# Three gating rows spread by transfers through memory in a two-layer decoder block on one Trainium2 core

## Chip, core and metric

The kernel runs on one core of one Trainium2 chip. The metric is the device time of one execution in microseconds; the time before is the median of three runs. In the text, PE is TensorE (PEld its weight load), DVE is VectorE, ACT is ScalarE, POOL is GpSimd, and SP is the sync engine, which here only issues transfers. Each engine works through its own instructions in order; a transfer issued by an engine stands in that engine's queue too, and an issue that waits for a semaphore holds up everything behind it there.

## The reference, cut to what matters

Two layers run over 512 tokens of width 1024. A vector `c` gives, for each layer, six modulation rows of 1024 numbers; two of them, `g1` and `g2`, gate what a mixer and an MLP add to the residual.

```python
c_act = jax.nn.silu(c)
for i in range(DEPTH):                                   # 2 layers
    mod = c_act @ ada_w[i] + ada_b[i]
    sh1, sc1, g1, sh2, sc2, g2 = jnp.split(mod, 6, axis=-1)
    h = modulate(rmsnorm(x, norm_mix_g[i]), sh1, sc1)
    y = pool_mixer(h, ...) if i == 0 else sgu_mixer(h, ...)
    x = x + g1[:, None, :] * y
    h = modulate(rmsnorm(x, norm_mlp_g[i]), sh2, sc2)
    x = x + g2[:, None, :] * (jnp.square(jax.nn.relu(h @ w1[i])) @ w2[i])
return rmsnorm(x, final_g)
```

Three of the four gating rows matter here: `g2` of layer 0 (in the code's column count, `c_g(1, 0)` of `mods[0]`), `g1` of layer 1 (`c_g(0, 0)` of `mods[1]`) and `g2` of layer 1 (`c_g(1, 0)` of `mods[1]`). The remaining one, `g1` of layer 0, is folded into the pooling weights and is not touched.

## The kernel before

Weights arrive as fp32, and every product is made of three fp32r products: `split` (lines 164 to 169) turns a weight tile into a high half `wh` (ACT, line 167) and a low half `wl` (DVE, line 168), and `mm3` (lines 174 to 178) issues wl times high, wh times low and wh times high. A raw weight tile of 512 KB lands in pool `w4`, which has three buffers; the halves `wh` and `wl` have five buffers each, so weights are made some products ahead of PE.

The modulation rows are computed on DVE, not on PE: `ada_tile` (line 190) loads a 128 x 1024 tile of `ada_w` into a buffer of `w4` (line 194) and reduces it against `cb`, the activated `c` on all partitions (line 198), into one column; after each second tile `finish_mods` (line 183) adds the bias and writes two columns of `mods[i]`. A gating row so stands in `mods` as 128 partitions x 8 columns: column k holds elements 128 k to 128 k + 127, one in each partition. But the gate is applied to tokens on the partitions (`gated`, line 964: `tmp = y * gb`), which needs the 1024 numbers along the free dimension, on all partitions: the tile `gb`, 128 x 1024, of which there is one for all three rows.

That is what `spread_cols` is for. `diagonals` (line 207, POOL) makes eight 128 x 128 tiles, each the identity scaled by one column; a product with a matrix of ones (line 216, PE, fp32, two of 128 x 512) sums over the partitions, so that every partition of the result holds all of the row; ACT evicts the two halves into `gb` (line 217). The 128 x 8 x 128 tile of scaled identities takes a buffer of `w4` in two cases, and one called `dgu` of pool `su` in the third.

The order of the stages and where the three spreads stand:

- Pooling mixer of layer 0, then the first MLP blocks (0 to some 90 us).
- MLP of layer 0. `mlp` (from line 595) walks a list `units`: "f" (first product and squared ReLU), "p" and, in layer 1, "s" (products arranged after Strassen's scheme), "q" (the last part). Beside the units it calls a list `extra` one by one at an even pace: eight `ada_tile` calls that finish `g2` of layer 0, the first spread, and 24 `ada_tile` calls for layer 1.
- SGU mixer of layer 1: two passes for `v`, its layer norm on DVE, then `do_u` and `do_mix` in a fixed order ("u0 u1 u2 u3 m0 u4 ..."); `do_u` pops up to three entries of `ex`, the first of which is the second spread. The product with `w_o` follows, with `gated` and eight more `ada_tile` calls.
- MLP of layer 1, which begins with four "f" blocks (`first1`; the transposes of `normed`, line 992, stand in the middle of them). The third spread's identities are made at the start, its products after the block `u == (0, 7)`. The weights of the "p" units come from loads and accumulating loads (`b_of`, line 761; `b_add`, line 765, on POOL).

PE's instructions stand in the order in which the program writes them (`manual_schedule(engines={PE})`). DVE, ACT, POOL and SP are in the program's order only in the opening part; later a list scheduler of the framework orders each of these queues, by its own estimate of durations, so a change in one place can move instructions elsewhere on them.

The input tiles' sources are named after the tensors: `in_ada` for `ada_w`, `in_w1f` for the first blocks of `w1` in layer 1, `in_w_v`, `in_w_u` (tile `ur`) and `in_w_o` for the SGU, `bt` and `b` for `w2`. Lines 1043 to 1045 load the layer norm's rows and the mixing weights of the SGU, one of them (`lnt`) as a broadcast of a row in memory to all partitions, which is the form of transfer that the change uses as well.

Of the kernel before, what the change touches and what calls it, by code (L numbers as in the profile page):

```python
# [7 lines left out]
F32 = mybir.dt.float32  # L8
F32R = mybir.dt.float32r
AF = mybir.ActivationFunctionType  # L10
ALU = mybir.AluOpType
# [3 lines left out]
P = 128  # L15
D = 1024
S = 512
KD = D // P
# [23 lines left out]
def c_sh(n, k):  # L42
    return 24 * n + 2 * k + 1


def c_g(n, k):
    return 24 * n + 16 + k
# [31 lines left out]
def decoder_kernel(ctx: ExitStack, tc: tile.TileContext, xtok, vecs, rows, fgrow, ada0, adag, ada1, pool_w, w1s, w1, w1f, w1b, w2, w2e, w_v, w_u, w_o, wsT, lnp, bs, out):  # L79
    nc = tc.nc  # L80
    V, A, G, T = nc.vector, nc.scalar, nc.gpsimd, nc.tensor
# [3 lines left out]
    w4 = ctx.enter_context(tc.tile_pool(name="w4", bufs=3))  # L85
# [20 lines left out]
    def bank(name, pool=None):  # L106
        pool = pool or ps
        return pool.tile([P, S], F32, name=name, tag="mm" if pool is ps else "xz")
# [4 lines left out]
    ones = cp.tile([P, P], F32, name="ones")  # L113
# [3 lines left out]
    ident = cp.tile([P, P], F32, name="ident")  # L117
    G.memset(ident, 0.0)
    G.affine_select(out=ident, in_=ident, compare_op=ALU.not_equal, fill=1.0, base=0, pattern=[[-1, P]], channel_multiplier=1)
    mods = [cp.tile([P, 48], F32, name=f"mods{i}") for i in range(2)]  # L120
# [16 lines left out]
    gb = big.tile([P, D], F32, name="gb")  # L137

    def X(t):
        return x_[t // 2][:, t % 2]  # L140

    def H(k, c):

        return h_[0][:, 0, k, c], h_[0][:, 1, k, c]
# [4 lines left out]
    def mod(i, c):  # L149
        return mods[i][:, c : c + 1]  # L150
# [30 lines left out]
    def finish_mods(i, b, pm):  # L181

        V.tensor_tensor(mods[i][:, 2 * b : 2 * b + 2], pm, vec[:, V_ADAB + 48 * i + 2 * b : V_ADAB + 48 * i + 2 * b + 2], ALU.add)
        n, q = divmod(b, 12)
        if q < 8:
            g0 = (V_MIX, V_MLP)[n] + 8 * i + q
            V.scalar_tensor_tensor(scl[i][n][:, q : q + 1], mod(i, 2 * b), 1.0, vec[:, g0 : g0 + 1], ALU.add, ALU.mult)
# [3 lines left out]
    def ada_tile(i, t, src, get):  # L191

        r = get()
        nc.sync.dma_start(r, src)
        b, j = divmod(t, 2)
        if j == 0:
            pmv[i, b] = sm.tile([P, 2], F32, name="pmv", tag="pmv")
        V.scalar_tensor_tensor(r, r, 1.0, cb, ALU.mult, ALU.mult, accum_out=pmv[i, b][:, j : j + 1])  # L198
        if j == 1:
            finish_mods(i, b, pmv.pop((i, b)))  # L200
# [1 line left out]
    def get4():  # L202
        return w4.tile([P, D], F32, name="ada", tag="w4")

    def diagonals(dg, cols):
        for k in range(KD):
            G.tensor_scalar(dg[:, k], ident, cols[:, k : k + 1], None, ALU.mult)

    def spread_cols(cols, dg=None):

        if dg is None:
            dg = w4.tile([P, KD, P], F32, name="dg", tag="w4")
            diagonals(dg, cols)
        for n in range(2):
            po = bank("pb")
            T.matmul(po, ones, dg[:, 4 * n : 4 * n + 4], start=True, stop=True)
            A.activation(gb[:, S * n : S * n + S], po, AF.Copy)


    def power(v, n):  # L220
# [12 lines left out]
    with (  # L233
# [67 lines left out]
        def rms():  # L301
            v0 = sm.tile([P, NT], F32, name="rv4", tag="rv4")
            V.tensor_scalar(v0, ss, RMS_EPS, None, ALU.add)
            rt.append(power(v0, NT))
# [285 lines left out]
    def parts(o, a):  # L590

        A.activation(o[0], a, AF.Copy)
        V.tensor_tensor(o[1], a, f32(o[0]), ALU.subtract)  # L593

    def mlp(i, first, extra, last, ending):
# [3 lines left out]
        with (  # L599
# [56 lines left out]
            def a_sums(step):  # L656


                def a(r, j):
                    return h32[0][:, 4 * j : 4 * j + 4, 256 * r : 256 * r + 256]  # L660

                def operand(pool, tag):
                    t = pool.tile([P, 2, 4, 256], F32R, name="as", tag=tag)
                    return t[:, 0], t[:, 1]

                def minus(o, p, q):
                    V.tensor_tensor(o, p, q, ALU.subtract)

                first, half = slice(0, 256), slice(256, 512)
                if step == 0:  # L670
                    sums_a.update({1: H(slice(0, 4), first), 2: H(slice(4, 8), first), 4: H(slice(4, 8), half)})
                    shift(hx, LINE - GAP)
                    minus(a(1, 1), a(1, 0), a(1, 1))
                    m, o = 5, operand(hx, "hx")
                elif step == 1:
                    minus(a(1, 1), a(1, 1), a(0, 0))
                    m, o = 6, operand(big, "x0")
                elif step == 2:
                    minus(a(0, 0), a(0, 0), a(1, 0))
                    V.tensor_tensor(a(1, 1), a(1, 1), a(0, 1), ALU.add)  # L680
                    m, o = 3, operand(big, "x1")
                else:
                    m, o = 7, H(slice(0, 4), half)
                parts(o, a(0, 0) if m == 7 else a(1, 1))
                sums_a[m] = o
# [214 lines left out]

            gain = mods[i][:, c_g(1, 0) : c_g(1, 0) + KD]
            done = first(put)
            if i:
                dg = su.tile([P, KD, P], F32, name="dgu", tag="u")
                diagonals(dg, gain)
            units = [("f", (0, f)) for f in range(done, 8)]
            for c in range(3):
                if i == 0:
# [17 lines left out]
            def ahead(n):  # L926

                if i == 0:
                    return min(n + 3, len(units))
                m, s = n + 1, items(*units[n])  # L930
                while m < len(units) and m < n + 5:
                    s += items(*units[m])
                    if s > 5 and m > n + 1:
                        break
                    m += 1
                return m
# [4 lines left out]
            for n, (kind, u) in enumerate(units):  # L941
                for m in range(n, ahead(n)):
                    if m not in ready:
                        ready[m] = prep[units[m][0]](units[m][1])
                while at < len(extra) and at < due * (n + 1):
                    extra[at]()
                    at += 1
                run[kind](u, ready[n])
                if i and kind == "f":
                    a_sums(u[1] - 4)  # L950
                    if u == (0, 7):
                        spread_cols(gain, dg)
                if i and u == (3, 1, 4):
                    reload()

# [24 lines left out]
    def normed(hf, i, n):  # L980

        xs = []
        for r in range(2):
            t = w4.tile([P, D], F32, name="xs", tag="w4")
            A.activation(t, X(2 * hf + r), AF.Copy, scale=rms(2 * hf + r))
            xs.append(t)
        c = slice(256 * hf, 256 * hf + 256)
        for k in range(0, KD, 2):
            px = bank("px")
            for q in range(2):  # L990
                for r in range(2):
                    T.transpose(px[:, 256 * q + P * r : 256 * q + P * r + P], xs[r][:, P * (k + q) : P * (k + q) + P], ident)
            tt = h32[0][:, k : k + 2, c] if h32 else sm.tile([P, 2, 256], F32, name="tt", tag="tmp")
            for q in range(2):
                a, b = scl[i][n][:, k + q : k + q + 1], mod(i, c_sh(n, k + q))
                if q:
                    A.activation(tt[:, q], px[:, 256:512], AF.Identity, bias=b, scale=a)
                else:
                    V.tensor_scalar(tt[:, q], px[:, 0:256], a, b, ALU.mult, ALU.add)
            parts(H(slice(k, k + 2), c), tt)  # L1000


    h32, xd = [], []
    dram = ctx.enter_context(tc.tile_pool(name="dram", bufs=1, space=bass.MemoryType.DRAM))

    def spill(h):
        xd.append(dram.tile([P, 2, D], F32, name=f"xd{h}"))
# [2 lines left out]
    def reload():  # L1010
        for h in range(2):
            x_[h] = big.tile([P, 2, D], F32, name=f"x{h}", tag=f"x{h}")
            G.dma_start(x_[h], xd[h])
        load_fg()
# [4 lines left out]
        return SWEEP  # L1019

    ex = [lambda q=q: ada_tile(0, 40 + q, ada1[q], get4) for q in range(8)]
    ex += [lambda: spread_cols(mods[0][:, c_g(1, 0) : c_g(1, 0) + KD])]
    ex += [lambda q=q: ada_tile(1, q, ada1[8 + q], get4) for q in range(24)]
    mlp(0, first0, ex, gated, lambda: normed(0, 1, 0))


# [6 lines left out]
    with (  # L1033
# [37 lines left out]
                V.tensor_tensor(v, v, lnt[:, n].rearrange("p (a b) -> p a b", a=2), op)  # L1071

        u, gt, wu = {}, {}, {}
        ex = [lambda: spread_cols(mods[1][:, c_g(0, 0) : c_g(0, 0) + KD])]
        ex += [lambda q=q: ada_tile(1, q, ada1[8 + q], get4) for q in range(24, 40)]

        def do_u(n):
# [75 lines left out]
    def last1(t, c0, n, src, y):  # L1153
# [13 lines left out]
        else:  # L1167
# [5 lines left out]
            nc.sync.dma_start(out[t, :, 1], X(t)[:, S:D])  # L1173

    mlp(1, first1, [], last1, lambda: None)


# [77 lines left out]
```

## Time and profile before

| | before |
|---|---|
| median of 3 runs | 876.26 us (875.87 to 877.03) |
| the profiled execution's own time | 876.84 us |
| its span | 875.1 us |
| PE busy | 858.3 us |
| DVE busy | 682.7 us |
| ACT busy | 449.6 us |
| POOL busy | 55.5 us |
| HBM read | 150.55 MB |

The page shows one execution on the chip. "Busy" is the time in which an engine had an instruction at work; matmuls overlap, so PE busy is not PE at its peak. The page also lists the groups of instructions by line, which the products of the spreads do not reach (they are among the smaller groups). The lines on which the argument rests stand in the prediction, in the part that uses them.

### The profile page before, as it was taken

How to read it: one execution, taken by the hardware profiler on the slowest of the kernel's cores; microseconds unless marked ns; L12 is line 12 of the kernel's file. 1: busy time of each engine (PE TensorE's matmuls, PEld its weight loads, DVE VectorE, ACT ScalarE, POOL GpSimd, SP SyncE). 2: the span in 40 equal slices, each digit the busy share in tenths (PEclk: the TensorE clock that was granted, in tenths of full speed). 3: DMA queues.
4: the chain of work that ended last, by engine and by line, in shares of the span. 5: the costliest groups of instructions: out<-in, count | busy, mean ns of one | idle time of the engine just before them, and what ended most of it. 6: DMA issues, size and time to landing. Idle time of an engine off the chain costs nothing. (4 is left out here: it accounts for less than half of the span.)

```text
span 875.1 us, 11762 instructions
## 1 busy us (share of the span) xinstructions
PE 858.3 (98%) x4580; PEld 739.1 (84%) x4580; DVE 682.7 (78%) x893; ACT 449.6 (51%) x653; POOL 55.5 (6%) x75
## 2 busy tenths in 40 slices
PE   8999999999999999999999999999999999999996
PEld 7778888788888888888878888999999988889885
DVE  6889696788869876657798866776877798778965
ACT  5285755554444445337233336665765575556621
POOL 3000002000000000000410012000000000000001
PEclk9999999999999999999999999999999999999999
DMA  9969843553554442514658526817464547456312
GB/s 348 417 233 310 299 175 122 192 192 129 184 201 160 145 145 72 193 65 177 214 170 266 169 97 224 305 31 188 121 201 126 139 130 247 102 140 216 122 47 97
DMA packets 37789, 155.51 MB, mean 178 GB/s; under 512 B 4195, under 2 KB 4323, under 8 KB 32486
## 3 DMA queue, kind: packets, MB, share of 16 engines
q1 hardware_dynamic: 35282, 137.72, 43.9%
q0 software_dynamic: 2304, 16.78, 8.9%
q8 instruction: 36, 0.59, 0.3%
q10 hardware_dynamic: 148, 0.27, 0.1%
q14 instruction: 19, 0.16, 0.1%
HBM read 150.55 MB, written 4.19 MB: 177 GB/s over the span
## 5 line engine op out<-in xcount | busy, mean ns | idle before, releaser
L176 PE MATMUL po<-hb,wl 128*128 128x256 f32 (+1 forms) x624 | 209.3, 335 | 1.3 <-DVE wl L168 1.3
L178 PE MATMUL po<-hb,wh 128*128 128x256 f32 (+1 forms) x624 | 207.6, 333 | 0.0
L177 PE MATMUL po<-hb,wh 128*128 128x256 f32 (+1 forms) x624 | 207.6, 333 | 0.0
L168 DVE TENSOR_TENSOR wl<-raw,wh 128x1024 fp32r<-128x1024 f32 x107 | 130.9, 1224 | 39.4 <-ACT wh L167 39.0
L167 ACT ACTIVATE wh<-raw 128x1024 fp32r<-128x1024 f32 x107 | 112.7, 1057 | 64.8 <-PE pm L178 28.6
L178 PE MATMUL pm<-wh,oh 128*128 128x512 f32 x336 | 130.7, 389 | 0.0
L177 PE MATMUL pm<-wl,oh 128*128 128x512 f32 x336 | 130.7, 389 | 0.0
L176 PE MATMUL pm<-wh,ol 128*128 128x512 f32 x336 | 130.7, 389 | 0.0
L176 PEld LDWEIGHTS po<-hb,wl 128*128 128x128 f32 x624 | 117.1, 188 | 14.6 <-DVE wl L168 1.7
L177 PEld LDWEIGHTS po<-hb,wh 128*128 128x128 f32 x624 | 117.2, 188 | 13.0 <-issue 0.7
L178 PEld LDWEIGHTS po<-hb,wh 128*128 128x128 f32 x624 | 118.0, 189 | 11.9
L168 DVE TENSOR_TENSOR wl<-b,wh 128x1024 fp32r<-128x1024 f32 x60 | 73.0, 1221 | 24.7 <-ACT wh L167 24.7
L198 DVE SCALAR_TENSOR_TENSOR ada<-ada,cb 128x1024 f32<-128x1024 f32 x56 | 68.3, 1223 | 15.7 <-DMA ada<-in_ada 15.5
L178 PEld LDWEIGHTS pm<-wh,oh 128*128 128x128 f32 x336 | 63.0, 188 | 13.2
L176 PEld LDWEIGHTS pm<-wh,ol 128*128 128x128 f32 x336 | 63.1, 188 | 12.3
L177 PEld LDWEIGHTS pm<-wl,oh 128*128 128x128 f32 x336 | 63.0, 188 | 12.3
L167 ACT ACTIVATE wh<-b 128x1024 fp32r<-128x1024 f32 x60 | 63.0, 1055 | 13.0 <-PE pm L178 6.7
L630 ACT ACTIVATE g<-po 128x512 f32<-128x512 f32 x40 | 23.6, 599 | 75.7 <-PE po L178 73.8
L969 ACT ACTIVATE tmp<-x 128x512 f32<-128x512 f32 (+1 forms) x25 | 15.3, 612 | 63.0 <-DVE x L965 63.0
L857 DVE TENSOR_TENSOR y<-y,pm 128x512 f32<-128x512 f32 x68 | 43.6, 682 | 0.0
L176 PE MATMUL po<-as,wl 128*128 128x256 f32 x144 | 40.7, 283 | 2.9 <-DVE wl L168 1.9
L168 DVE TENSOR_TENSOR wl<-bt,wh 128x1024 fp32r<-128x1024 f32 x24 | 28.9, 1222 | 17.5 <-ACT wh L167 17.5
(211 smaller groups left out, 1491.0 us busy)
## 6 DMA issues: line engine op xcount, KB each, us to landing
ada<-in_ada SPq DMA_DIRECT2D x72, 512.0 KB, 3.3
b<-in_w SPq DMA_DIRECT2D x21, 1024.0 KB, 4.9
raw<-in_w SPq DMA_DIRECT2D x25, 512.0 KB, 3.9
raw<-in_w1b SPq DMA_DIRECT2D x24, 512.0 KB, 5.0
bt<-in_w POOLq DMA_DIRECT2D x9, 1024.0 KB, 8.3
raw<-in_w2e SPq DMA_DIRECT2D x16, 512.0 KB, 3.3
wh<-in_ada SPq DMA_DIRECT2D x9, 512.0 KB, 9.6
wl<-in_ada SPq DMA_DIRECT2D x9, 512.0 KB, 9.9
```

What stands on the lines that cost most here:

```text
L167: A.activation(h, r, AF.Copy)
L168: V.tensor_tensor(l, r, f32(h), ALU.subtract)
L176: T.matmul(o, wl, mh, start=first, stop=False, **kw)
L177: T.matmul(o, wh, ml, start=False, stop=False, **kw)
L178: T.matmul(o, wh, mh, start=False, stop=last, **kw)
L198: V.scalar_tensor_tensor(r, r, 1.0, cb, ALU.mult, ALU.mult, accum_out=pmv[i, b][:, j : j + 1])
L630: A.activation(t, po, AF.Relu)
L857: V.tensor_tensor(yt, yt, banks[hf], ALU.subtract if minus else ALU.add)
L969: A.activation(tmp, xt, AF.Square, scale=D**-0.5, accum_out=s[:, len(cs) : len(cs) + 1])
```

## The change

`spread_cols` now stores the eight columns into a row in device memory (`dram.tile([KD, P])`, one for each of the three spreads) with the two dimensions exchanged, and then loads that row into all partitions of `gb` with a broadcast. Both transfers are issued on SP's queue. The products, the scaled identities with their buffers, and the evictions are gone. The first spread's call moves within `extra` from behind the eighth `ada_tile` to behind the twelfth; the other two stand at the same calls as before. The pool `dram`, which the kernel already used for `spill`, is opened earlier.

```diff
-    def diagonals(dg, cols):
-        for k in range(KD):
-            G.tensor_scalar(dg[:, k], ident, cols[:, k : k + 1], None, ALU.mult)
-
-    def spread_cols(cols, dg=None):
-
-        if dg is None:
-            dg = w4.tile([P, KD, P], F32, name="dg", tag="w4")
-            diagonals(dg, cols)
-        for n in range(2):
-            po = bank("pb")
-            T.matmul(po, ones, dg[:, 4 * n : 4 * n + 4], start=True, stop=True)
-            A.activation(gb[:, S * n : S * n + S], po, AF.Copy)
+    dram = ctx.enter_context(tc.tile_pool(name="dram", bufs=1, space=bass.MemoryType.DRAM))
+
+    def spread_cols(cols, name):
+
+        line = dram.tile([KD, P], F32, name=name)
+        nc.sync.dma_start(line.rearrange("k p -> p k"), cols)
+        nc.sync.dma_start(gb, line.rearrange("(o k) p -> o (k p)", o=1).to_broadcast([P, D]))
...
-            if i:
-                dg = su.tile([P, KD, P], F32, name="dgu", tag="u")
-                diagonals(dg, gain)
...
                     if u == (0, 7):
-                        spread_cols(gain, dg)
+                        spread_cols(gain, "gain1")
...
     ex = [lambda q=q: ada_tile(0, 40 + q, ada1[q], get4) for q in range(8)]
-    ex += [lambda: spread_cols(mods[0][:, c_g(1, 0) : c_g(1, 0) + KD])]
     ex += [lambda q=q: ada_tile(1, q, ada1[8 + q], get4) for q in range(24)]
+    ex.insert(12, lambda: spread_cols(mods[0][:, c_g(1, 0) : c_g(1, 0) + KD], "gain0"))
     mlp(0, first0, ex, gated, lambda: normed(0, 1, 0))
...
-        ex = [lambda: spread_cols(mods[1][:, c_g(0, 0) : c_g(0, 0) + KD])]
+        ex = [lambda: spread_cols(mods[1][:, c_g(0, 0) : c_g(0, 0) + KD], "gainm")]
         ex += [lambda q=q: ada_tile(1, q, ada1[8 + q], get4) for q in range(24, 40)]
```

More of the change, by code (lines that the diff above doesn't have):

```diff
@@ L1003, in decoder_kernel @@
     h32, xd = [], []
-    dram = ctx.enter_context(tc.tile_pool(name="dram", bufs=1, space=bass.MemoryType.DRAM))
     def spill(h):
```

## The prediction

> **What bounds the kernel now.** I read the page first, then the waits of PE, then the busy time by stage, then single rows in order of time. In the rows of a timeline the columns are start, duration, engine, line, operation and tiles, count, and in brackets the idle time before with what ended it; "SPq" is an issue by SP's queue.
>
> ```profile
> span 875.1 us, 11762 instructions
> PE 858.3 (98%) x4580; PEld 739.1 (84%) x4580; DVE 682.7 (78%) x893; ACT 449.6 (51%) x653; POOL 55.5 (6%) x75
> ```
> ```profile
> PE po L176 <- DVE wl L168: 3.1, 3, 1.3
> ```
> ```profile
> 431.00:501.00 70.00, 70.00 (x339) 58.44 (x338) 63.50 (x107) 23.85 (x32) 4.38 (x4) 1.00 0.63 208
> 540.00:560.00 20.00, 19.87 (x175) 19.87 (x176) 13.30 (x19) 12.44 (x19) 3.19 (x5) 1.00 0.95 338
> ```
>
> TensorE is the bound: 98% busy, its longest kind of wait after the opening is 3.1 us in three pieces, and the granted clock is 1.00 in both stretches shown (columns there: stretch, length, then busy PE, PEld, DVE, ACT, POOL, clock, DMA share, GB/s). So time taken off PE's queue comes off the end, unless what feeds PE cannot come earlier. Two stages have such feeders close behind: from 431 to 501 us VectorE is busy 63.5 of 70 us, and from 540 to 560 us the DMA engines are 95% busy.
>
> **What the change removes.** Each of the three spreads is two fp32 products, which PE runs as four passes between two weight products.
>
> ```profile
> 157.26 0.39 PE L178 MATMUL pm<-wh,oh 128*128 128x512 f32 x1
> ...
> 157.94 0.40 PE L178 MATMUL pm<-wh,oh 128*128 128x512 f32 x1
> 158.18 1.88 PE L216 MATMUL pb<-dg,ones 128*128 128x512 f32 x4
> 159.50 0.79 PE L176 MATMUL po<-hb,wl 128*128 128x512 f32 x1
> 160.12 0.40 PE L177 MATMUL po<-hb,wh 128*128 128x512 f32 x1
> ```
> ```profile
> 446.13 0.40 PE L178 MATMUL po<-hb,wh 128*128 128x512 f32 x1
> ...
> 448.31 0.40 PE L177 MATMUL po<-hb,wh 128*128 128x512 f32 x1
> ```
> ```profile
> 585.09 0.28 PE L178 MATMUL po<-hb,wh 128*128 128x256 f32 x1
> ...
> 585.43 0.28 PE L178 MATMUL po<-hb,wh 128*128 128x256 f32 x1
> ...
> 587.38 0.28 PE L177 MATMUL po<-hb,wh 128*128 128x256 f32 x1
> ```
>
> Undisturbed, three 512-wide products start in 157.94 - 157.26 = 0.68 us, so 0.227 each; 256-wide ones in (585.43 - 585.09) / 3 = 0.113. From the last product before a spread to the second one after it there are two such steps. First spread: 160.12 - 157.94 - 0.45 = 1.73 us. Second: 448.31 - 446.13 - 0.45 = 1.73. Third: 587.38 - 585.43 - 0.23 = 1.72. Sum on PE: **5.18 us**. Two slots of PSUM per spread and 24 products on POOL go too, and ScalarE loses six evictions, all beside PE; I give them nothing of their own.
>
> **What it adds: six transfers on SP's queue.** Each spread becomes a store of the 128 x 8 gate columns into a row in memory, whose last step is one 4-byte word (1024 packets, 64 for each of 16 engines), and a load of that row to all partitions (128 x 4 KB), which waits for the store to land and for the last reader of gb. SP is in order, so everything behind them waits too. No row shows a 4-byte packet. The nearest:
>
> ```profile
> q1 hardware_dynamic: 35282, 137.72, 43.9%
> ...
> q10 hardware_dynamic: 148, 0.27, 0.1%
> ```
>
> The columns are packets, MB and share of 16 engines' span. A packet of q1 (3.9 KB) holds an engine for 0.439 x 16 x 875.1 / 35282 = 174 ns, one of q10 (1.8 KB) for about 95 ns. A line through both leaves 26 ns for a packet without bytes; with q10's rounded share at 0.15% it leaves 114. Bounds: nothing, and 174 ns, which is 64 x 0.174 = 11.1 us for a store. I take 40 ns, near the line's end and a little above for that rounding: **2.6 us** in which the rings pass nothing that was issued behind it.
>
> The Trainium skill, "DMA: Bandwidth & Descriptors", says in "Rules for kernel authors" that a last dimension that isn't contiguous becomes one descriptor per element, and in "Specifications" that the engines read, modify and write below 512 B. Its table of measured loads under "Bandwidth" has about 10.5 ns for each packet over all engines at the smallest size; by that, as an estimate, 1024 packets take 10.8 us, which is the upper bound again and speaks against the change.
>
> **First spread (gain0).** In the built order its store stands behind the ninth gather of the stage and ahead of the tenth.
>
> ```profile
> 137.39 0.16 DVE L183 TENSOR_TENSOR mods<-pmv,vec 128x2 f32<-128x2 f32 x1
> ...
> 149.07 1.23 DVE L593 TENSOR_TENSOR ol<-u,oh 128x1024 fp32r<-128x1024 f32 x1 [1.98 <-ACT oh L592]
> ```
> ```profile
> 147.12 0.33 SPq L194 DMA_DIRECT2D ada<-in_ada  x1
> ...
> 155.65 1.07 ACT L167 ACTIVATE wh<-raw 128x1024 fp32r<-128x1024 f32 x1 [0.65 <-PE pm L178]
> ```
>
> The columns are ready at 137.5, while the ninth gather's load was issued at 147.1, because the scaled identities held one of three w4 buffers. That buffer is now free, so the two new transfers use time in which SP only waited. What is late next is the tenth gather, on VectorE ahead of the ol of 149.07. ScalarE's split at 155.65 waited for PE to hand back a buffer, so weights are made ahead of their use; a few us of delay are covered. Price 0; at the upper bound the gather would hold VectorE some 8 us and I would expect a stall of 1 to 2.
>
> **Second spread (gainm).** The store follows the wsbs loads, the load follows two ur loads.
>
> ```profile
> 356.56 0.58 SPq L1045 DMA_DIRECT2D wsbs<-in_bs  x1
> 373.34 19.69 SPq L155 DMA_DIRECT2D raw<-in_w_v  x4
> ...
> 401.35 6.02 SPq L155 DMA_DIRECT2D raw<-in_w_v  x4
> ```
> ```profile
> 397.76 0.69 DVE L964 TENSOR_TENSOR tmp<-y,gb 128x512 f32<-128x512 f32 x1
> ```
>
> SP issues nothing from 357.1 to 373.3, 16 us, above the store's upper bound; gb's last read ends at 398.5, before SP's next issue at 401.4. Price 0. But this stage has VectorE as close feeder:
>
> ```profile
> 500.28 0.69 DVE L1104 TENSOR_TENSOR gtl<-u,gth 128x512 fp32r<-128x512 f32 x1 [0.70 <-ACT gth L1103]
> ```
> ```profile
> 502.26 0.39 PE L176 MATMUL po<-wh,gtl 128*128 128x512 f32 x1
> ```
>
> The last gtl ends at 500.97 and PE takes it at 502.26: 1.29 us of slack, while PE comes 1.73 earlier. VectorE's order is changed here: two of the gathers (1.15 us each) now run before the second split of ur, not after it, which leaves less for the end of the chain. I take 0; bounds 0 and about 2 us, all of this spread's gain and a little more.
>
> **Third spread (gain1).** Its store stands behind three loads of w1f and ahead of bt and the fourth load of w1f; this is the tight place.
>
> ```profile
> 538.56 0.16 DVE L183 TENSOR_TENSOR mods<-pmv,vec 128x2 f32<-128x2 f32 x1
> ...
> 547.30 1.23 DVE L168 TENSOR_TENSOR wl<-raw,wh 128x1024 fp32r<-128x1024 f32 x1 [3.54 <-ACT wh L167]
> 549.06 1.90 DVE L999 TENSOR_SCALAR h<-px,scl,mods 128x256 f32<-128x256 f32 x4 [0.53 <-PE px L992]
> ...
> 553.16 1.29 DVE L593 TENSOR_TENSOR hb<-h,hb 128x512 fp32r<-128x512 f32 x2 [0.66 <-ACT hb L592]
> ```
> ```profile
> 538.90 0.33 SPq L761 DMA_DIRECT2D bt<-in_w  x1
> 540.10 0.33 SPq L155 DMA_DIRECT2D raw<-in_w1f  x1
> ```
> ```profile
> 546.20 1.06 ACT L167 ACTIVATE wh<-raw 128x1024 fp32r<-128x1024 f32 x1 [0.60 <-DMA raw<-in_w1f]
> ```
> ```profile
> 550.08 0.37 PE L176 MATMUL po<-hb,wl 128*128 128x256 f32 x1
> ...
> 555.05 0.28 PE L177 MATMUL po<-hb,wh 128*128 128x256 f32 x1
> ```
>
> The store can go at 538.7, just ahead of bt. The fourth load is what ScalarE waits for at 546.2; VectorE's split of it ends at 548.53, PE wants it at 550.08: slack 1.55. Behind that split VectorE has the scaling at 549.06 (idle 0.53 before it) and the last low half, which ends at 554.45 and is used at 555.05, slack 0.60. So a delay X of that load costs PE about X - 1.1. With X = 2.6: **1.5 us**; with the bounds 0 and 10.0. The broadcast load and two loads of b behind it are wanted later, and what feeds 563 onward was split 5 us ahead; nothing for those.
>
> **Sum.** The profiled execution took 876.84 us (875.1 span and 1.7 around it); the median of the runs is 876.26. 876.84 - 5.18 + 1.5 = 873.2 in that execution's terms, and 876.26 - 3.7 = **872.6** for the median.
>
> **The rivals.**
> 1. The store is cheap, X below 1.1: all 5.18 us stay, 871.1. For it: 4 KB in all, and the line's 26 ns (1.7 us) is not far above. Against: 64 packets per engine.
> 2. VectorE becomes the bound from 431 to 501: the second saving is lost, with up to 0.3 more for gathers that wait in its queue, on top of my sum: 872.6 + 2.0 = 874.6. For it: 63.5 of 70 busy, 1.29 us slack. Against: the moved gathers.
> 3. Slower: the 4-byte packets cost what whole packets cost. At 174 ns the fourth load of w1f is 11.1 us late, PE stands 10.0 us at 550, and the sum is 876.26 - 5.18 + 10.0 = 881.1. It decides from X - 1.1 = 5.18 + 1.75, X = 8.0 us or 125 ns a packet, above the 114 of the line with q10 rounded up. Against it: two kinds of packet suggest that time falls with size. The skill's 10.5 ns (above) would end here, at 880.8 as an estimate.
>
> **How the numbers follow.** My forecast has 0.38 (its own range 871.3 to 874.2, X from 1.3 to 4.2), rival 1 0.15, rival 2 0.17, rival 3 0.22, and 0.08 lies between forecast and rival 3 with no change to tell. What can be told from no change is 0.2%, 1.75 us: faster means below 874.5, slower above 878.0. Rival 2 lies on the line, half and half. Faster 0.38 + 0.15 + 0.09 = 0.62, same 0.08 + 0.08 = 0.16, slower 0.22. The range from 870.6 to 879.5 leaves out a good half of rival 3.
>
> **What would show it.** Right: no L216 on PE, the step from L178 to L177 back at 0.45 us at those three places; PE's start at gt's product about 3.5 us earlier; a stall of 1 to 2 us at the fourth w1f block, with ScalarE waiting longer for that load. Step by step wrong: the store landing in under 3 us or over 8; a stall at the first mixing or the last gtl; SP's w_v loads later than 373 less 1.7; PE idle near 150 to 170. The prediction fails altogether if PE's idle time grows by over 5 us anywhere.

## The result, and the profile after

| | before | after |
|---|---|---|
| median of the runs | 876.64 us (875.87 to 878.36, 4 runs) | 885.26 us (883.25 to 886.68, 4 runs) |
| profiled execution: time, span | 876.84, 875.1 us | 886.36, 884.7 us |
| PE busy | 858.3 us | 856.7 us |
| DMA packets under 512 bytes | 4195 | 7363 |

The kernel became slower: ratio 1.009, 95% interval 1.007 to 1.0109. Line numbers shift a little: the store is line 210, the broadcast load 211, b's loads 755. First the page of the changed kernel, then its table of PE's waits (total in us, times, longest).

```profile
span 884.7 us, 11709 instructions
...
PE 856.7 (97%) x4568; PEld 740.1 (84%) x4568; DVE 680.8 (77%) x893; ACT 446.0 (50%) x647; POOL 34.4 (4%) x51
```
```profile
PE po L176 <- DVE wl L168: 14.5, 4, 10.8
```

PE works less than before, and the span is 9.6 us longer: most of the time went into one wait, 10.8 us long, for a low half of a weight. The next rows, in order of time on SP's queue, ScalarE, VectorE and PE of the changed kernel, follow it back.

```profile
535.17 0.38 SPq L210 DMA_DIRECT2D gain<-mods  x1
535.66 0.52 SPq L755 DMA_DIRECT2D bt<-in_w  x1
536.60 0.33 SPq L155 DMA_DIRECT2D raw<-in_w1f  x1
547.23 0.33 SPq L211 DMA_DIRECT2D gb<-gain  x1
```
```profile
555.17 1.06 ACT L167 ACTIVATE wh<-raw 128x1024 fp32r<-128x1024 f32 x1 [13.27 <-DMA raw<-in_w1f]
```
```profile
556.26 1.23 DVE L168 TENSOR_TENSOR wl<-raw,wh 128x1024 fp32r<-128x1024 f32 x1 [16.19 <-ACT wh L167]
```
```profile
557.54 0.58 PE L176 MATMUL po<-hb,wl 128*128 128x256 f32 x1 [10.82 <-DVE wl L168]
557.92 0.41 PE L177 MATMUL po<-hb,wh 128*128 128x256 f32 x1
...
561.95 0.29 PE L178 MATMUL po<-hb,wh 128*128 128x256 f32 x1
562.07 0.28 PE L176 MATMUL po<-hb,wl 128*128 128x256 f32 x1
...
562.66 0.28 PE L178 MATMUL po<-hb,wh 128*128 128x256 f32 x1
```

The fourth load of w1f is issued at 536.60, right behind gain1's store and bt. ScalarE can split it at 555.17, 18.57 us later; before, issue and split were 6.10 us apart (540.10 and 546.20). So the load came 12.5 us late, and everything behind it on ScalarE, VectorE and PE with it. Behind the stall the products start every 0.21 us, not 0.113, for 4.4 us. The stretches of the changed kernel (busy us of PE, PEld, DVE, ACT, POOL, then granted clock, DMA share, GB/s) show both halves of it. The DMA share counts a packet's whole time in the stretch in which it starts, so it can pass 1.

```profile
536.00:538.00 2.00, 1.47 (x12) 1.48 (x13) 2.00 (x3) 1.17 (x2) 0.00 (x0) 1.00 2.81 68
538.00:540.00 2.00, 2.00 (x20) 2.00 (x19) 2.00 (x4) 1.16 (x3) 0.58 (x1) 1.00 0.03 4
540.00:542.00 2.00, 2.00 (x20) 2.00 (x20) 0.07 (x1) 1.76 (x2) 0.55 (x1) 1.00 1.15 45
542.00:544.00 2.00, 2.00 (x20) 2.00 (x19) 0.00 (x0) 0.00 (x0) 0.00 (x0) 1.00 0.75 25
544.00:546.00 2.00, 2.00 (x20) 2.00 (x19) 0.00 (x0) 0.00 (x0) 0.00 (x0) 1.00 0.36 20
546.00:548.00 2.00, 0.71 (x7) 0.48 (x5) 0.00 (x0) 0.00 (x0) 0.00 (x0) 1.00 0.87 139
...
550.00:552.00 2.00, 0.00 (x0) 0.00 (x0) 0.00 (x0) 0.00 (x0) 0.00 (x0) 0.91 1.04 426
552.00:554.00 2.00, 0.00 (x0) 0.00 (x0) 0.00 (x0) 0.00 (x0) 0.00 (x0) 0.50 0.98 410
...
560.00:562.00 2.00, 2.00 (x12) 2.00 (x11) 1.35 (x3) 1.98 (x5) 0.00 (x0) 0.53 0.95 330
```

From 538 to 546 us next to no data moves (4 to 45 GB/s), though two loads of 1.5 MB together have been issued; they run from 546 on, at over 400 GB/s from 550. The first of their packets had started: the 2.81 of the row from 536 to 538 is that. In the packet records of the kept trace the sixteen 8 KB packets of bt that start then take 3.1 to 9.5 us each, where 0.31 us is usual. And the granted clock of PE falls to 0.50 some 5 us after PE went idle, and is back 4 to 5 us after it resumed. The Trainium skill, "TensorE: Matmul & The Clock Gate", section "What's actually happening", gives half the clock after an idle window of about 3.4 us and the full clock after as long a busy one; these rows agree with the half, and in the times roughly.

The sum: 876.84 - 5.18 (the products, as predicted) + 10.82 (stall) + 2.15 (20 products between 557.54 and 561.95, which took 4.41 us and not 20 x 0.113) = 884.6, against 886.36 of this execution. Of the 1.7 us left, some 1.3 lie from 562 to 596 us, where the products start every 0.118 us ((562.66 - 562.07) / 5) and not 0.113, at the full granted clock. The first run below, which has no stall, shows the same 0.118 there, and the runs with the store on ScalarE's queue and with the store twice, which have the stall, show 0.113. So the stall is not its cause; what is stays open. From median to median, 876.64 to 885.26, the same terms leave 0.8 us.

### The profile page after: what moved, and what is told of

The parts are those of the page before. It is cut to its first block, busy times and chain, and to the rows that moved or that the text cites. A ratio compares the mean times of both kernels' runs of the same rounds, so it can differ in the third digit from the quotient of the medians.

```text
span 884.7 us, 11709 instructions
## 1 busy us (share of the span) xinstructions
PE 856.7 (97%) x4568; PEld 740.1 (84%) x4568; DVE 680.8 (77%) x893; ACT 446.0 (50%) x647; POOL 34.4 (4%) x51
## 2 busy tenths in 40 slices
DMA packets 41341, 157.09 MB, mean 178 GB/s; under 512 B 7363, under 2 KB 7491, under 8 KB 36038
```

## The experiments

All runs are compared with the kernel before on the same chip (876.87 to 877.29 us). "Fourth load" is the time from the issue of the fourth w1f load to ScalarE's split of it: 6.1 us before, 18.6 after.

**gain1 alone undone**, with products and scaled identities as before:

```diff
-                        spread_cols(gain, "gain1")
+                        spread_products(dg)
...
```

> The third spread (gain1) is made by products and scaled identities again; the other two stay transfers. Theory A (the whole loss is gain1's store, whose 1024 packets stand ahead of the fourth load of w1f): no stall at the fourth w1f block, two savings of 1.73 us kept, 876.6 - 3.5 = 873.2 us (872.3 to 874.3), PE's clock 1.00 throughout. Rival C (the other two stores cost as well, through the gathers behind them): the stall of about 11 us may go, but the time stays above 875.

Measured 873.74 us (ratio 0.9966, 0.9953 to 0.9978), fourth load 6.0 us, no stall. The loss lies in gain1; the other two transfers keep their two savings.

**The store at another time.** The columns pass through an instruction that waits for a late result.

```diff
-                        spread_cols(gain, "gain1")
+                        late = sm.tile([P, KD], F32, name="late", tag="late", bufs=1)
+                        V.scalar_tensor_tensor(late, g[0, 1][:, 2, 0:KD], 0.0, gain, ALU.mult, ALU.add)
+                        spread_cols(late, "gain1")
```

> All three spreads by transfers; gain1's columns are first added to zero times a late result, so that the same 1024-packet store is issued some 40 us later, behind three loads of w1b, where the DMA engines of the changed kernel were 1 per cent busy (580 to 600 us). Theory A: the fourth w1f load lands about 6 us after its issue again, no stall at 545, all 5.2 us kept: 876.6 - 5.2 = 871.4 us (870.7 to 872.6). Rival B (not the store, but that bt and the fourth load are issued 3.5 us earlier than before, into loads that are still landing): a stall of over 5 us stays, 879 or more. Should the late store hurt a load behind it: 873 to 878, with a wait at the first w1b block.

Measured 881.71 us (1.0042 to 1.0067), a miss: the stall at 545 was gone, but the stage from 150 to 350 us had become slower, long before the edit's place. The same edit with the columns in a dead part of `mods` (and waiting for `g[0, 1][:, 1, 0:KD]`):

> gain1's store late again, but its 128 x 8 columns go into a dead part of mods instead of a new tile, so every other tile keeps its address. Theory A (the place of the store decides, and the first late version lost its gain to the 32 bytes by which its new tile shifted the tiles behind it): 222 products per 50 us between 150 and 350 us again, not 219, no stall at 545, 876.9 - 5.2 = 871.7 us (870.5 to 874.0, the upper part if the load behind the store is still late at the first w1b blocks near 618). Rival (the slower products came from the late store or its wait, not from addresses): 219 per 50 us again and 880 or more.

Measured 874.36 us (0.9957 to 0.9977). One stretch of each, the first version and then the second:

```profile
150.00:350.00 200.00, 200.00 (x871) 163.22 (x871) 161.80 (x188) 95.88 (x116) 0.00 (x0) 1.00 0.45 160
```
```profile
150.00:350.00 200.00, 200.00 (x884) 165.59 (x883) 164.49 (x192) 97.09 (x118) 0.00 (x0) 1.00 0.46 165
```

At the same clock PE got through 871 instructions, and then 884. Up to the edit's place the two traces have the same instructions in the same order on PE, VectorE, ScalarE, GpSimd and SP, so what differs there is where tiles lie: the new tile of 32 bytes moves tiles behind it. That this is the cause is argued so, not shown, and which tile's address it is stays open. For it speaks that the kernel itself pads its pools to set offsets in lines of 128 words (`shift`, line 95), and that the new tile `turned` of the last run below, which is just 128 words a partition, leaves the 884. In the second version the fourth load, issued at 536.34 as early as in the changed kernel, took 6.0 us: the early issue does not make the stall, the store does. SP's queue here also shows what a packed store takes where the DMA engines have nothing else to do, since the broadcast load waits for it to land:

```profile
576.79 0.38 SPq L210 DMA_DIRECT2D gain<-mods  x1
587.50 0.33 SPq L211 DMA_DIRECT2D gb<-gain  x1
587.92 16.98 SPq L155 DMA_DIRECT2D raw<-in_w1b  x4
```
```profile
576.00:580.00 4.00, 4.00 (x38) 4.00 (x37) 1.99 (x3) 2.07 (x3) 0.00 (x0) 1.00 0.12 1
580.00:584.00 4.00, 4.00 (x38) 4.00 (x37) 1.67 (x2) 3.09 (x4) 0.00 (x0) 1.00 0.00 0
```

10.7 us for 4 KB, and hardly any of it in the DMA engines: their share of 0.12 in the first stretch is 0.12 x 16 x 4 = 7.7 us over all engines, some 7 ns for each of the 1024 packets and 0.5 us for each engine. From 580 to 584 us nothing is in the engines, and the store has still not landed. The w1b load at 587.92 waited behind it, and PE stood 0.62 and 1.05 us near 613 and 622; these stand for a part of the 2.7 us by which the time lies over 871.7.

**The same bytes in longer pieces.**

```diff
-        nc.sync.dma_start(line.rearrange("k p -> p k"), cols)
+        if name == "gain1":
+            nc.sync.dma_start(line.rearrange("k p -> (k p)").rearrange("(p k) -> p k", k=KD), cols)
...
```

> gain1's store stays at its place with the same 4 KB, but goes to memory partition by partition: 128 pieces of 32 bytes instead of 1024 of 4 (the last gate is so applied in another order of columns). Theory A with a price per packet: 12.5 us / 8 = 1.6 us, the fourth w1f load 1 to 3 us late, a stall of 0 to 2 us, 871.4 to 873.5 us. Rival (a fixed price of a store to memory, or the place itself): stall of about 11 us, 883 to 887.

Measured 873.07 us (0.9942 to 0.9972), fourth load 6.6 us. Place, queue and bytes are those of the changed kernel; only the pieces are 32 bytes long (gb then holds the columns in another order; this version leaves out putting them right). The broadcast load was issued 1.93 us after the store here:

```profile
535.47 0.33 SPq L211 DMA_DIRECT2D gain<-mods  x1
...
537.40 0.33 SPq L214 DMA_DIRECT2D gb<-gain  x1
```

**The store on ScalarE's queue.**

```diff
-        nc.sync.dma_start(line.rearrange("k p -> p k"), cols)
+        (nc.scalar if name == "gain1" else nc.sync).dma_start(line.rearrange("k p -> p k"), cols)
```

> gain1's store of 1024 pieces is issued on ScalarE's queue instead of SP's, the rest is the same. If what stands in the way is the order of one queue (the load waits behind the store in SP's ring), the fourth w1f load lands some 6 us after its issue and the time is 871.4 to 873. If the small packets take the DMA engines themselves, whatever queue they come from, the load stays 5 to 12 us late: stall of 4 to 11 us, 876 to 886.

Measured 883.21 us (1.0062 to 1.0089), fourth load 17.1 us, stall 9.2. The order within one queue is not what holds the load back. The Trainium skill, "DMA: Bandwidth & Descriptors", section "Issuing engines are not separate DMA queues", says that transfers of all issuing engines share the same DMA engines, and this run agrees.

**The clock apart from the stall.** Products whose result is overwritten, ahead of the fourth w1f block:

```diff
                     normed(1, 1, 1)
                     spill(1)
+                    for _ in range(84):
+                        T.matmul(pos[n - 1][:, 256:512], wf[0][0][:, 0], H(0, c)[0], start=True, stop=True)
```

> The changed kernel with 84 products of 256 columns (9.5 us at 0.113) put into PE's queue ahead of the fourth w1f block; their result is overwritten. Theory A says that the loss has a second term, the granted clock of 0.50 for 5 us after the stall (44 products lost half their speed, some 2 to 2.5 us): PE idles about 1.3 us only, the clock stays at 1.00, 885.3 - 2.3 = 883 us (882 to 884). Rival (the low clock is only recorded, or comes from the late data): 885 to 886. If the filling ends later than the load's landing: 886 or more.

Measured 882.01 us (1.0046 to 1.0077), 3.25 us below the changed kernel. PE and its clock in this run:

```profile
546.48 10.14 PE L1134 MATMUL po<-hb,wh 128*128 128x256 f32 x84
556.62 0.38 PE L176 MATMUL po<-hb,wl 128*128 128x256 f32 x1
556.84 0.29 PE L177 MATMUL po<-hb,wh 128*128 128x256 f32 x1
...
557.53 0.28 PE L177 MATMUL po<-hb,wh 128*128 128x256 f32 x1
```
```profile
550.00:556.00 6.00, 6.00 (x54) 6.00 (x53) 0.66 (x1) 1.06 (x1) 0.00 (x0) 1.00 1.03 425
```

The block began 0.92 us earlier than in the changed kernel (its load came 0.9 us sooner), and the clock stayed at 1.00; with the 2.15 of the sum above that makes 3.1. The changed kernel's executions lie as far apart as that (883.25 to 886.68), so the time alone does not prove the term. The rows do: behind the filling the products start every (557.53 - 556.84) / 6 = 0.115 us and not every 0.21, so the low clock is a real second term.

**Twice the store.** A second line in memory gets the same columns, right behind the first.

```diff
         nc.sync.dma_start(line.rearrange("k p -> p k"), cols)
+        if name == "gain1":
+            twin = dram.tile([KD, P], F32, name="twin")
+            nc.sync.dma_start(twin.rearrange("k p -> p k"), cols)
```

> The changed kernel with gain1's columns stored twice, the second time into a line that nobody reads: 1024 more 4-byte pieces ahead of bt and the fourth load of w1f. Theory A at 10.5 ns a piece ((11.3 to 12.0 us) - 1.9 for 896 pieces more than in the run with 32-byte pieces): the fourth load lands 10.8 us later still, PE stands 21 to 22 us at 545, 885.3 + 10.8 = 896 us (894 to 899). Rival (stores overlap each other, the time is one of latency): 886 to 889.

Measured 884.88 us (1.0071 to 1.0112), fourth load 17.2 us: a miss. 2048 words cost what 1024 cost, so the price is not one of words or packets in a row, as theory A had it.

**Strided gates.** All stores in 32-byte pieces, and the gating products read gb with a stride of 8 words.

```diff
+        line = dram.tile([P, KD], F32, name=name)
+        nc.sync.dma_start(line, cols)
+        nc.sync.dma_start(gb, line.rearrange("(o p) k -> o (p k)", o=1).to_broadcast([P, D]))
+    def gate(o, a, c0, n):
+        k, p = gb.rearrange("q (p k) -> q k p", k=KD), "q (k p) -> q k p"
+        V.tensor_tensor(o.rearrange(p, p=P), a.rearrange(p, p=P), k[:, c0 // P : (c0 + n) // P], ALU.mult)
...
```

> All three stores write 128 pieces of 32 bytes, and the gating products on VectorE read gb with a stride of 8 words, so the outputs are in their proper order. Theory A: each store lands about 2 us after its issue instead of 9 to 12, no stall at the fourth w1f block, 871.7 us (870.5 to 873.5), if a strided read costs VectorE nothing (0.69 us each). Rival: strided reads are slower; at twice 0.69 us for 26 of them VectorE has 18 us more, of which the last three in the end of the kernel show: 873 to 876.

Measured 875.63 us (0.9969 to 0.9988): no stall at the fourth w1f block, but the time is the rival's: strided reads are slower. The other half of the expectation missed in part as well, since only gain1's store landed after some 2 us: the broadcast loads were issued 3.7 us (gain0) and 2.4 us (gain1) after the stores, and gainm's store took 8.9 us to land. The gating products of this run, min, median and max in ns:

```profile
L215 DVE TENSOR_TENSOR tmp<-y,gb x15: 1122/1147/1171, 354.7 to 859.4; 128x512 f32<-128x512 f32 x15
```

They took 1.15 us and not 0.69. The Trainium skill, "SBUF — State Buffer", has a note on lines of 16 bytes in its section "Door 1: The DMA port swizzle", by which a step past such a line costs; the step here was 32 bytes, and the row agrees. That this alone makes the 2 to 3 us by which the run lies over the one before with 32-byte pieces was not shown.

**What makes a packed store slow.** The kernel with gain1 by products, plus a dead store at the place of the changed kernel's, whose layout in memory varies (16 in the tile's last dimension for words 64 bytes apart, 128 for 512, 2 for 8):

```diff
+                        apart = dram.tile([P, KD, 16], F32, name="apart")
+                        nc.sync.dma_start(apart[:, :, 0], gain)
```

> The run with gain1's spread by products (873.7 us, no stall at the fourth w1f block), plus a store of the same 1024 4-byte words at the place where the changed kernel has it, which nobody reads, its words 64 bytes apart in memory instead of next to one another. Theory H1 (the pieces are slow because many write into the same few lines of memory, one after the other; the doubled store cost nothing more since it went to other lines): the fourth load lands 6 to 8 us after its issue, stall under 2 us, 873.5 to 876. Theory H2 (a price of each small piece in the path of the store, wherever it goes): stall of about 11 us, 883 to 888.

> The same with the words 512 bytes apart. H1 with lines of any size up to 512 bytes: 873.5 to 876, also where 64 bytes apart is still slow. H2: 883 to 888.

Half of a packed store:

```diff
+                        apart = dram.tile([KD, P], F32, name="apart")
+                        nc.sync.dma_start(apart[4:8].rearrange("k p -> p k"), gain[:, 4:8])
```

> The same dead store at that place with four of the eight columns (512 words, next to one another). If the price goes by the pieces of one store (H1 or H2): half of some 10 us more than a store of 32-byte pieces, the fourth load lands about 12 us after its issue, stall of 4 to 6 us, 878 to 881. H3 (a fixed price of a store with 4-byte pieces, which would explain why a second one cost nothing): stall of about 11 us, 883 to 888.

The packed control, the changed kernel's order with words 64 and 16 bytes apart (`dram.tile([KD, P, 16])` and `[KD, P, 4]`), and words 8 bytes apart in the other order:

> Control for the stores that nobody reads: gain1's spread by products, plus the dead store of 1024 words in the form of the changed kernel (eight rows of 512 bytes, neighbours in a row come from neighbouring partitions), with no broadcast load behind it. All theories with the price in the store: stall of 9 to 11 us at the fourth w1f block and the low clock behind it, 884 to 887. If the broadcast load of gb had a part in it: 878 to 882.

> The dead store with the same order of rows and partitions and the same form of issue (128 x 8 x 1) as in the changed kernel, only that the words lie 64 bytes apart. H1 (neighbouring words in a line of memory are written one after the other): as with the other scattered stores, no stall over 1.5 us, 873.5 to 876. H4 (the scattered stores were cheap since they were issued in another form, 1024 x 1 x 1, and another order): stall of 9 to 11 us, 884 to 887.

> The dead store with the words 8 bytes apart, partition by partition: eight words of one partition share 64 bytes. H1 with a price by words in a 64-byte line, whoever writes them: half of the packed store's, the fourth load some 4 to 6 us late, stall of 3 to 5 us, 877 to 880. If only words from different partitions disturb one another: like the scattered stores, 873.5 to 876.

> The dead store in the changed kernel's order with the words 16 bytes apart: four words from four partitions share 64 bytes, 32 share 512. H1 with a price by the words in a line: a quarter of some 9 us on top of the 3 of a scattered store, the fourth load 4 to 6 us late, stall of 2 to 4 us, 876 to 879. H1 with a price of sharing at all: stall of 9 to 11 us, 884 to 887. Shared lines without a price: 873.5 to 876.

| dead store | words in 64 bytes | fourth load, us | stall, us | time, us | ratio, 95% |
|---|---|---|---|---|---|
| none | | 6.0 | 0 | 873.74 | 0.9953 to 0.9978 |
| 1024 words, 512 apart | 1 | 9.1 | 1.63 | 874.73 | 0.9967 to 0.9987 |
| 1024, 64 apart | 1 | 8.6 | 1.11 | 875.69 | 0.9973 to 0.9991 |
| 1024, 64 apart, changed kernel's order | 1 | 8.2 | 0.45 | 874.97 | 0.9963 to 0.9983 |
| 1024, 16 apart, the same order | 4 | 9.5 | 1.71 | 875.46 | 0.9970 to 0.9988 |
| 1024, 8 apart | 8 | 14.0 | 6.56 | 882.79 | 1.0045 to 1.0079 |
| 1024 packed | 16 | 17.3 | 9.56 | 886.26 | 1.0090 to 1.0120 |
| 512 packed | 16 | 16.7 | 8.87 | 884.51 | 1.0072 to 1.0103 |

The rows behind two of its lines, packed first and then 64 apart in the same order:

```profile
537.44 0.33 SPq L155 DMA_DIRECT2D raw<-in_w1f  x1
```
```profile
554.77 1.06 ACT L167 ACTIVATE wh<-raw 128x1024 fp32r<-128x1024 f32 x1 [11.90 <-DMA raw<-in_w1f]
```
```profile
536.81 0.33 SPq L155 DMA_DIRECT2D raw<-in_w1f  x1
```
```profile
545.00 1.06 ACT L167 ACTIVATE wh<-raw 128x1024 fp32r<-128x1024 f32 x1 [2.80 <-DMA raw<-in_w1f]
```

Both issue 1024 words in the same form and order; 17.3 and 8.2 us. The scattered words are no quicker in the DMA engines than the packed ones above. This is the 64-apart run, in the stretch in which its store's packets pass:

```profile
536.00:537.00 1.00, 0.28 (x2) 0.28 (x3) 1.00 (x2) 1.00 (x2) 1.00 (x1) 1.00 0.47 4
```

0.47 x 16 x 1 = 7.5 us over all engines, as much as the 7.7 of the packed store. So the difference of 9 us arises after the store's packets have passed the engines. The packed control keeps the whole stall without a broadcast load, so that load has no part in it. The price follows the nearness of the words in memory: over the run without a store it is 2 to 3 us where each word has 64 bytes for itself, 3.5 with four in 64 bytes, 8.0 with eight and 11.3 with sixteen. Half or twice as many words at the same nearness cost the same (10.7 and 11.2). A reading that fits is that places in memory are written side by side and the words of one place after one another, some 0.7 to 1 us for each at eight and sixteen. That is argued, not shown, and the dose is not an even one: eight words in 64 bytes cost more than the half of the packed price that had been expected (882.79 us against 877 to 880), and four cost hardly more than one (875.46 us, in the range written down for no price of sharing). The half store missed the range for a price by pieces and lies in the one for a fixed price (884.51). Eight words of one partition disturb each other as well, so it takes no second partition. Open is how large such a place is: one larger than 64 bytes, in which the share of words written went along, was not told apart, nor was the total stretch of memory that a store covers. Open too is why the packets of large loads last so long meanwhile.

**Columns turned on PE first.** PE turns the columns to 8 x 128 first, and a store has 8 pieces of 512 bytes.

```diff
-        nc.sync.dma_start(line.rearrange("k p -> p k"), cols)
+        po = bank("pb")
+        T.transpose(po[0:KD, 0:P], cols, ident)
+        turned = sm.tile([P, P], F32, name="turned", tag="turned", bufs=1)
+        A.activation(turned[0:KD], po[0:KD, 0:P], AF.Copy)
+        nc.sync.dma_start(line, turned[0:KD])
```

> All three spreads by transfers, but PE turns the 128 x 8 columns into 8 x 128 first (one small transpose each, an eviction by ScalarE), so a store writes 8 pieces of 512 bytes. The third one stands where the products stood, behind the loads of w1f. Theory A: store lands in 2 to 4 us, no stall at 545, PE keeps 5.2 us less about 0.3 for each transpose: 876.9 - 4.3 = 872.6 (871.5 to 874.5), VectorE's gating at 0.69 us. Rival (PE waits for a column or for an eviction at the transposes): 875 to 877.

Measured 872.22 us (ratio 0.9950, 0.9937 to 0.9962), fourth load 6.5 us. Store and broadcast load are 1.23 us apart. The third store stands behind the fourth load here, so the missing stall alone does not speak for the longer pieces; the 1.23 us do. A transpose costs PE 190.95 - 190.39 - 0.45 = 0.11 us:

```profile
583.05 0.29 SPq L214 DMA_DIRECT2D gain<-turned  x1
584.28 0.34 SPq L215 DMA_DIRECT2D gb<-gain  x1
```
```profile
190.39 0.39 PE L178 MATMUL po<-hb,wh 128*128 128x512 f32 x1
190.62 0.27 PE L211 MATMUL pb<-ident,mods 128*8 128x128 f32 x1
...
190.95 0.39 PE L177 MATMUL po<-hb,wh 128*128 128x512 f32 x1
```

## Why the prediction was wrong, step by step

- **The products removed: right.** 5.18 us was the sum. The last product of `w_o`, the end of the stage behind the first two spreads, began at 538.48 before and begins 3.57 us earlier now, where 3.46 was worked out (rows below, before and after); the run with only those two saved 3.3 us.

```profile
538.48 0.39 PE L178 MATMUL po<-wh,gth 128*128 128x512 f32 x1
```
```profile
534.91 0.39 PE L178 MATMUL po<-wh,gth 128*128 128x512 f32 x1
```

- **gain0 at price 0: right.** Its packed store landed after 9.6 us (the broadcast load went at 147.40, the store at 137.76), near the upper bound. The tenth gather came late and VectorE stood 7.13 us, but PE was busy for all of that stretch (second fence below, 150 to 165 us): the weights made ahead covered even the 1 to 2 us that I had allowed for at that bound.

```profile
137.76 0.39 SPq L210 DMA_DIRECT2D gain<-mods  x1
147.40 0.33 SPq L211 DMA_DIRECT2D gb<-gain  x1
147.83 0.39 SPq L194 DMA_DIRECT2D ada<-in_ada  x1
```
```profile
150.00:165.00 15.00, 15.00 (x68) 12.43 (x67) 10.70 (x13) 6.38 (x8) 0.00 (x0) 1.00 0.70 255
```
```profile
154.18 1.23 DVE L198 SCALAR_TENSOR_TENSOR ada<-ada,cb 128x1024 f32<-128x1024 f32 x1 [7.13 <-DMA ada<-in_ada]
```

- **gainm at price 0: right.** The store landed after 12.5 us in SP's 16 us without an issue (355.49 to 371.52), and the 3.57 us above leave nothing for rival 2, VectorE as the bound. Here the pieces are not the whole price: in 32-byte pieces the store took 8.9 us at this place, where the second wsbs load ahead of it took 9.2 (12.5 and 9.3 here).

```profile
355.49 0.69 SPq L210 DMA_DIRECT2D gainm<-mods  x1
371.52 19.70 SPq L155 DMA_DIRECT2D raw<-in_w_v  x4
```
```profile
gainm<-mods SPq DMA_DIRECT2D x1, 4.0 KB, 12.5
```

- **gain1: place and path right, the delay X wrong in kind and in size.** This is the step that failed. "Ahead of the fourth load of w1f", "a delay X costs PE about X - 1.1" held: X was 12.5, and the stall 10.8 where that gives 11.4. But X had been taken as 2.6, the time that 64 packets of 40 ns hold an engine, and the true X lay above even the bound of 11.1. Sum and bound both took the packets' time in the engines for the store's time. The runs show some 7 ns a packet and 0.5 us an engine, and then 10 us until words that lie side by side in memory have landed, in which the load behind them hardly moves. A row for 4-byte packets would not have helped: the page before counts 4195 packets under 512 bytes, nearly all of them 4 bytes long and 9 ns in the trace's packet records, which would have given 0.6 us. That 2.6 us lies within what scattered words cost (2.2 to 3.1) is chance.
- **A term left out.** The granted clock of 0.50 behind the stall, 2.15 us; the filling run bears it out. A stall long enough costs more than its length: the stall of 6.6 us, of the words 8 bytes apart, was followed by a clock of 0.50 too, the one of 1.6 us, of those 512 apart, was not.
- **Rival 3 has the path and nearly the time**, 881.1 without that term, with the deciding point at X = 8.0, but not the mechanism: its 174 ns a packet came near X by luck. It had been held at 0.22 because time seemed to fall with a packet's size, which is so (7 ns here) and decides nothing. The estimate of 10.8 us from the Trainium skill's 10.5 ns a packet ("DMA: Bandwidth & Descriptors", "Bandwidth") came close to X too, and yet the runs do not bear it out as a price of each packet: 512, 1024 and 2048 packed words cost alike, and 1024 scattered ones about a quarter of that.

## What to carry to other kernels

A transfer that turns columns into a row in memory with 4-byte words side by side took 9 to 13 us here for 4 KB, and loads issued after it, on another queue too, stood nearly still. Turn the data on chip first (0.11 us on PE), and the store took 1.2 us; in 32-byte pieces it took 1.9 to 3.7 us where no other slow transfer stood beside it. The time that a transfer's packets hold the engines (0.5 us here) is not the time until it lands. Where a small operation has no row in the trace, bound it by its kind and not by its bytes, and look first at what waits right behind it: two of these three stores were free only because weights lay ready for PE or the queue had nothing else to issue. And add to a stall of PE that lasts over some 5 us the products that then run at half the clock.

## What the runs showed that was not expected

- 1024 words of 4 bytes cost the load behind them 11.3 us packed, 8.0 with 8 bytes from word to word, and 2.2 to 3.5 from 16 bytes on; the number of packed words (512, 1024, 2048) made no difference. Packed or scattered, the packets held the DMA engines for the same 7 ns or so each.
- With a new tile of 32 bytes a partition, PE's products were slower by 1.5% (871 instead of 884 instructions in 200 us) at the full granted clock; the order of instructions was the same, so moved addresses are the likely cause.
- In some executions the products of one stretch start every 0.118 us instead of 0.113 at the full granted clock, with or without a stall; the cause is open.
- Reading one operand with a step of 32 bytes took VectorE from 0.69 to 1.15 us for 128 x 512.
